# Expert routing and expert loop of one hybrid layer: fused sum on VectorE, pair sums beside the scores, a reordered loop

## The chip, the cores and the metric

One Trainium2 chip, and of it one core. The metric is the device time of one execution in microseconds (us). The core's engines run their own instruction streams in order: TensorE (PE, with its weight loads PEld), VectorE (DVE), ScalarE (ACT), GpSimd (POOL) and SyncE (SP, which here issues most loads). They wait for each other by semaphores.

## What is computed

One layer: an input projection into three groups of heads, an output projection, and then a product-key expert network (PEER) over 512 tokens, d = 1024, 16384 experts. The change lies in the last part alone. Cut to it, the reference is

```python
q = (t @ w_q).reshape(n_tok, 8, 2, 128)                      # 8 heads, two halves
s = einsum('thid,hikd->thik', q, sub_keys)                   # scores against 128 keys per half
v1, i1 = top_k(s[:, :, 0], 16); v2, i2 = top_k(s[:, :, 1], 16)
cand = v1[..., :, None] + v2[..., None, :]                   # 256 sums per head
top_s, pos = top_k(cand, 16)
idx = (i1 * 128 + i2) at pos                                 # 128 experts per token
g = softmax(top_s)
act = gelu(einsum('tkd,td->tk', u_tab[idx], x))
out = einsum('tk,tkd->td', g * act, v_tab[idx])
```

followed by a gated residual and an RMSNorm.

## The kernel before, in words

The 512 tokens are four tiles of 128. Tile 3 gathers its expert rows: 128 times, an indirect DMA issued by GpSimd (`g_load`, L1511) brings one row of u and v (2048 numbers) to each of 128 partitions; DVE takes the dot with the token (`g_dot`, L1516), ACT the gelu of that column (`g_act`, L1519), DVE multiplies the column by the gate (`g_weight`, L1522: wG), ACT scales the v half by it (L1526) and GpSimd adds it to `accG` (L1528). The buffers `row` are four.

Tiles 0 to 2 (384 tokens) take the dense way: for each of 128 groups of 128 experts ("an expert" below) PE computes a u block of 24 matmuls over 384 columns (`u_block`, tile pu), ACT the gelu, DVE multiplies by the dense gate weights gd (L1684), and PE adds the v products, 18 matmuls over 512 columns, into six PSUM accumulators (`e_v`, tile pv). To keep precision each f32 operand is split: ACT copies the high part (`wh`, L177), another engine subtracts to get the low part (`wl`, L180), and three matmuls replace one (L187 to L189). `wwh` and `wwl` are the parts of the weighted activations. 70 of the 128 u blocks, the list `AHEAD`, are computed before the loop: two with the norm, nine beside the scores, and the others by the generator `ahead_steps`, which is stepped by `go_ahead` and from inside the weights stage. Their activations go to DRAM (`act_d`) and come back as `acl`. At depth 2 a step loads and splits pieces up to two steps ahead and issues low parts a step later; the engine of the low parts is `u_eng`, GpSimd until L1617 sets it to DVE.

The stages, in order. Scores: for 16 half heads `hi`, PE computes queries and scores, DVE takes the best 16 per tile (`top16`: MAX8, FIND_INDEX8, MATCH_REPLACE8, twice). In this stage PE and GpSimd follow the written order, and a scheduler places the other engines' instructions. From there on everything follows the written order. Routing: for the tiles 3, 0, 1, 2 the pair sums (`top_pairs`: seven small sums over all eight heads into `cand`, then a `top16` per head), then `route`, which turns positions into expert indices by wide comparisons and products (tiles eq and sel, 128x2048), with the Exp of the softmax on ACT (L1459); seven steps of `ahead_steps` per tile stand between, and two after. Weights: 48 rounds (`weights_T`), in which DVE makes masks (oi, ow), PE multiplies them into gate weights (768 matmuls of 128 columns, gdps), ACT copies these out, and in 36 of the rounds a step of `ahead_steps` is taken; 12 rows of the gather lie here. Expert loop: step i issues the loads of expert i + 4, the dot, gelu and gate of a row, splits u of i + 2 and v of i + 1, computes the u block of i + 1 and weights it, then the row's sum, then the v products of i. 116 rows lie here.

Of the kernel before, what the change touches and what calls it, by code (L numbers as in the profile page):

```python
# [17 lines left out]
P = 128  # L18
# [132 lines left out]
def build(tc, A, out, dbg=None):  # L151
# [1057 lines left out]
    FIRST = [(0, 1), (1, 0), (1, 1), (2, 0)]  # L1209
# [136 lines left out]
    tk = tkp.sb("tk1", side="right")  # L1346
    scp = Pools()
# [40 lines left out]
    def top_pairs(t):  # L1388

        cd = cds[t % 2]  # L1390
        v1, v2 = vv_[t][:, :, 0, :], vv_[t][:, :, 1, :]

        def block(c0, nj, j1, n0, n):

            o = cd[:, :, c0:c0 + 16 * nj].rearrange("p h (j n) -> p h j n", n=16)[:, :, :, n0:n0 + n]
            V.tensor_tensor(o, v2[:, :, n0:n0 + n].unsqueeze(2).broadcast_to([P, 8, nj, n]),
                            v1[:, :, j1:j1 + nj].unsqueeze(3).broadcast_to([P, 8, nj, n]), ALU.add)

        def row(c0, j1, n0, n):
            V.tensor_tensor(cd[:, :, c0:c0 + n], v2[:, :, n0:n0 + n], v1[:, :, j1:j1 + 1].broadcast_to([P, 8, n]), ALU.add)  # L1400
# [6 lines left out]
        V.tensor_tensor(cd[:, :, 128:136], v1[:, :, 8:16], v2[:, :, 0:1].broadcast_to([P, 8, 8]), ALU.add)  # L1407
        for hh in range(8):
            top16(ts_a[t][:, hh, :], pos_a[t][:, hh, :], cd[:, hh, :], 136, tk2)

    psO = scp.ps("psO2", bufs=3)
# [33 lines left out]
    order.enter_context(tc.manual_schedule())  # L1445
    u_depth[0] = 2
    rtp = Pools()
    tk2 = rtp.sb("tk2", bufs=2, side="right")
# [3 lines left out]
    def route(t):  # L1452
# [6 lines left out]
        S.activation(e, e, AF.Exp)  # L1459
# [14 lines left out]
        for i, jj in ((0, j1), (1, j2)):  # L1474
# [14 lines left out]
            if i == 0:  # L1489
                yield  # L1490
# [29 lines left out]

    def g_weight(k):
        V.tensor_tensor(wG[:, k:k + 1], actG[:, k:k + 1], gG[:, k:k + 1], ALU.mult)  # L1522

    def g_acc(k):
        row = rows.pop(k)
        S.activation(row[:, D:2 * D], row[:, D:2 * D], AF.Copy, scale=wG[:, k:k + 1])  # L1526
        if k:
            G.tensor_tensor(accG, accG, row[:, D:2 * D], ALU.add)  # L1528
        else:
            G.tensor_copy(accG, row[:, D:2 * D])  # L1530
# [18 lines left out]
    def weights_T(t):  # L1549
        for q8 in range(16):  # L1550
# [66 lines left out]
    u_eng[0] = V  # L1617
# [26 lines left out]
    ac, ww, gw, sqs, fss = {}, {}, {}, {}, {}  # L1644

    def e_load(a):
        if a in AHEAD:
            ac[a] = gl.tile([P, TD], F32, name="acl")
            nc.sync.dma_start(ac[a], act_d[AHEAD.index(a)])
        elif (a, 0) not in ld:  # L1650
            e_fetch(a, 0)
        if (a, 1) not in ld:
            e_fetch(a, 1)

    def e_split_u(a):
        if (a, 0) not in sp:
            e_split(a, 0)

    def e_split_v(a):
        if (a, 1) not in sp:  # L1660
            e_split(a, 1)
# [175 lines left out]
```

## Time and profile before

| what | us |
|---|---|
| median of three runs (2030.21 to 2032.35) | 2030.38 |
| the profiled execution | 2030.01 |
| its span, first to last instruction | 2028.2 |
| PE busy in the span | 1887.1 (93%) |
| DVE busy | 1516.8 (75%) |
| ACT busy | 932.7 (46%) |
| GpSimd busy | 914.9 (45%) |
| mean granted clock of TensorE | 0.972 of full speed |

The trace gives start and length of each instruction, and for an idle time the event that ended it. A matmul's length is modelled, and matmuls overlap in the pipeline, so the distance from one start to the next tells their pace. The chain of work that ended last lies by 36% on PE, by 29% on DVE and by 17% on issue, time in which an engine waited for nothing that the profile shows.

### The profile page before, as it was taken

How to read it: one execution, taken by the hardware profiler on the slowest of the kernel's cores; microseconds unless marked ns; L12 is line 12 of the kernel's file. 1: busy time of each engine (PE TensorE's matmuls, PEld its weight loads, DVE VectorE, ACT ScalarE, POOL GpSimd, SP SyncE). 2: the span in 40 equal slices, each digit the busy share in tenths (PEclk: the TensorE clock that was granted, in tenths of full speed). 3: DMA queues.
4: the chain of work that ended last, by engine and by line, in shares of the span. 5: the costliest groups of instructions: out<-in, count | busy, mean ns of one | idle time of the engine just before them, and what ended most of it. 6: DMA issues, size and time to landing. Idle time of an engine off the chain costs nothing.

```text
span 2028.2 us, 26813 instructions
## 1 busy us (share of the span) xinstructions
PE 1887.1 (93%) x9703; PEld 1546.4 (76%) x9703; DVE 1516.8 (75%) x2604; ACT 932.7 (46%) x1491; POOL 914.9 (45%) x458
## 2 busy tenths in 40 slices
PE   7999998879998999888999799999999999999997
PEld 4777866556777889888999677777787878778775
DVE  5552179986535456998899878888888888888885
ACT  4332233426544333433777645455445445444444
POOL 1004046740013543564122256576666575675653
PEclk9999999989999999989999789999999999999999
DMA  9546232145313433464787698888888998888971
GB/s 339 166 135 206 63 114 63 42 153 185 96 65 107 147 113 107 132 229 136 246 291 281 230 381 308 313 311 315 304 318 316 354 330 303 317 318 294 323 268 59
DMA packets 209044, 445.20 MB, mean 220 GB/s; under 512 B 13296, under 2 KB 135920, under 8 KB 190960
## 3 DMA queue, kind: packets, MB, share of 16 engines
q1 hardware_dynamic: 171616, 258.47, 39.0%
q0 software_dynamic: 18432, 134.23, 17.4%
q10 hardware_dynamic: 18864, 50.80, 6.7%
q8 instruction: 76, 1.25, 0.2%
q14 instruction: 56, 0.46, 0.1%
HBM read 394.02 MB, written 51.51 MB: 220 GB/s over the span
## 4 chain that ended last, share of the span: by engine, by line
PE 36%; DVE 29%; issue 17%; ACT 8%; DMA 6%; POOL 3%; ACTq 0%; DVEq 0%; SPq 0%; POOLq 0%
DVE wl L180 10%; DVE row L1516 6%; PE acc L187 4%; PE acc L189 4%; PE acc L188 4%; PE pu L189 3%; PE pu L187 3%; PE pu L188 3%; POOL wl L180 3%; ACT wwh L177 3%; DMA wraw<-in_peer_ut 2%; DVE oi L1557 2%; ACT wh L177 2%; DVE ow L1561 1%; PE acc L419 1%
## 5 line engine op out<-in xcount | busy, mean ns | idle before, releaser
L1528 POOL TENSOR_TENSOR accG<-accG,row 128x1024 f32<-128x1024 f32 x127 | 358.7, 2825 | 383.8 <-ACT row L1526 379.3
L180 DVE TENSOR_TENSOR wl<-wraw,wh 128x1024 fp32r<-128x1024 f32 x268 | 339.5, 1283 | 149.0 <-ACT wh L177 140.4
L177 ACT ACTIVATE wh<-wraw 128x1024 fp32r<-128x1024 f32 x324 | 335.1, 1051 | 227.3 <-PE acc L188 80.0
L189 PE MATMUL pu<-u2h,wl 128*128 128x384 f32 (+2 forms) x1040 | 360.9, 347 | 15.1 <-DVE wl L180 12.7
L187 PE MATMUL pu<-u2h,wh 128*128 128x384 f32 (+2 forms) x1040 | 359.3, 346 | 16.0 <-ACT act L1303 14.6
L188 PE MATMUL pu<-u2l,wh 128*128 128x384 f32 (+2 forms) x1040 | 354.8, 341 | 0.0
L187 PE MATMUL pv<-wh,wwh 128*128 128x512 f32 x768 | 310.0, 404 | 25.1 <-ACT wwh L177 24.8
L189 PE MATMUL pv<-wh,wwl 128*128 128x512 f32 x768 | 309.7, 403 | 0.0
L188 PE MATMUL pv<-wl,wwh 128*128 128x512 f32 x768 | 303.7, 395 | 0.0
L1522 DVE TENSOR_TENSOR wG<-actG,gG 128x1 f32<-128x1 f32 x128 | 223.2, 1744 | 33.0 <-ACT actG L1519 33.0
L1511 POOL DMA_INDIRECT row<-in_peer_uv,idxG x128 | 210.9, 1648 | 36.2 <-POOL accG L1528 33.1
L189 PEld LDWEIGHTS pu<-u2h,wl 128*128 128x128 f32 x1040 | 199.8, 192 | 32.2 <-DVE wl L180 28.1
L180 POOL TENSOR_TENSOR wl<-wraw,wh 128x1024 fp32r<-128x1024 f32 x56 | 143.7, 2570 | 166.3 <-ACT wh L177 139.6
L187 PEld LDWEIGHTS pu<-u2h,wh 128*128 128x128 f32 x1040 | 200.3, 193 | 20.2 <-ACT act L1303 15.9
L187 PEld LDWEIGHTS pv<-wh,wwh 128*128 128x128 f32 x768 | 144.9, 189 | 76.6 <-ACT wwh L177 49.7
L188 PEld LDWEIGHTS pu<-u2l,wh 128*128 128x128 f32 x1040 | 200.2, 193 | 2.5
L189 PEld LDWEIGHTS pv<-wh,wwl 128*128 128x128 f32 x768 | 144.7, 188 | 48.5 <-DVE wwl L180 16.6
L188 PEld LDWEIGHTS pv<-wl,wwh 128*128 128x128 f32 x768 | 144.9, 189 | 29.6 <-issue 0.2
L1516 DVE CUSTOM_DVE_ANT_0 row<-row,u2G 128x1024 f32<-128x1024 f32 x128 | 156.1, 1219 | 0.0
L1526 ACT ACTIVATE row<-row,wG 128x1024 f32<-128x1024 f32 x128 | 145.7, 1138 | 4.7 <-ACT act L1303 3.8
L177 ACT ACTIVATE wwh<-acl 128x384 fp32r<-128x384 f32 x70 | 36.7, 525 | 197.0 <-DVE acl L1684 197.0
L1571 ACT ACTIVATE stg<-gdps 128x512 f32<-128x512 f32 x96 | 96.8, 1137 | 17.7 <-PE gdps L1569 17.3
(412 smaller groups left out, 3346.0 us busy)
## 6 DMA issues: line engine op xcount, KB each, us to landing
wraw<-in_peer_ut SPq DMA_DIRECT2D x128, 512.0 KB, 4.6
wraw<-in_peer_uv SPq DMA_DIRECT2D x128, 512.0 KB, 6.3
gd_d<-stg ACTq DMA_DIRECT2D x12, 2048.0 KB, 8.4
gd<-gd_d SPq DMA_DIRECT2D x31, 768.0 KB, 9.1
wraw<-in_w_in SPq DMA_DIRECT2D x36, 512.0 KB, 4.1
acl<-act_d SPq DMA_DIRECT2D x70, 192.0 KB, 5.6
act_d<-act ACTq DMA_DIRECT2D x68, 192.0 KB, 3.8
kT<-in_ada_w SPq DMA_DIRECT2D x18, 512.0 KB, 4.6
```

Of the source, the lines that this page charges most:

```text
L177: S.activation(hi, full, AF.Copy)
L180: (eng or V).tensor_tensor(lo, full, hi.bitcast(F32), ALU.subtract)
L187: PE.matmul(ps, ah, bh, start=start, stop=False)
L188: PE.matmul(ps, ah, bl, start=False, stop=False)
L189: PE.matmul(ps, al, bh, start=False, stop=stop)
L1511: G.indirect_dma_start(out=rows[k], out_offset=None, in_=A["peer_uv"], in_offset=bass.IndirectOffsetOnAxis(ap=idxG[:, k:k + 1], axis=0))
L1516: V.tensor_tensor_reduce(row[:, 0:D], row[:, 0:D], u2G, 1.0, 0.0, ALU.mult, ALU.add, actG[:, k:k + 1])
L1522: V.tensor_tensor(wG[:, k:k + 1], actG[:, k:k + 1], gG[:, k:k + 1], ALU.mult)
L1526: S.activation(row[:, D:2 * D], row[:, D:2 * D], AF.Copy, scale=wG[:, k:k + 1])
L1528: G.tensor_tensor(accG, accG, row[:, D:2 * D], ALU.add)
L1557: V.tensor_tensor(oi.rearrange("p w g b c -> p (w g) b c"), iotaA.unsqueeze(1).broadcast_to([P, 8, P, 2]), tb(ixT), ALU.is_equal)
L1571: S.activation(stg[:, :, t0:t0 + 4].rearrange("p a t -> p t a"), ps, AF.Copy, scale=1.0 / GSCALE)
```

## The change

Four things are changed. The row's sum: ACT makes wG as a scaled copy, and DVE one fused multiply-add into `accG`; ACT's scaling of the row and GpSimd's addition are gone. The pair sums: `top_pairs` works on a group of heads, and the table `PAIRS` puts four, then two heads of each tile behind later scores; the last two heads follow the scores, with one u block per tile; the buffers `sc` are four instead of three. The low parts: `u_eng` becomes DVE right behind those last pair sums (26 low parts change engine), the Exp is issued after the first half of `route`, and three steps of `ahead_steps` per tile are left out of the routing's loop (22 u blocks stand in the routing instead of 30, and 37 in the weights stage instead of 29). The expert loop: loads run six (u) and four (v) experts ahead, gate weights five, u is split three ahead and its block computed two ahead; the high parts are issued first, then the low parts, and the row's gelu and sum stand behind them.

```diff
-    FIRST = [(0, 1), (1, 0), (1, 1), (2, 0)]
+    FIRST = [(1, 0), (0, 1), (3, 0), (1, 1)]
...
         for t in range(NX):
             top16(vv_[t][:, hh, i, :], ix_[t][:, hh, i, :], sc[:, t, :], P, sc2)
+        if hi in PAIRS:
+            for t, h0, nh in PAIRS[hi]:
+                top_pairs(t, h0, nh)
...
+    PAIRS = {8: [(3, 0, 4)], 9: [(0, 0, 4)], 10: [(1, 0, 4)], 11: [(2, 0, 4)],
+             12: [(3, 4, 2)], 13: [(0, 4, 2)], 14: [(1, 4, 2), (2, 4, 2)]}
...
     u_depth[0] = 2
+    for t in (3, 0, 1, 2):
+        top_pairs(t, 6, 2)
+        go_ahead(1)
+    u_eng[0] = V
...
         V.tensor_tensor(e, ts, ts[:, :, 0:1].broadcast_to([P, 8, 16]), ALU.subtract)
-        S.activation(e, e, AF.Exp)
...
             if i == 0:
+                S.activation(e, e, AF.Exp)
                 yield
...
     def g_act(k):
         S.activation(actG[:, k:k + 1], actG[:, k:k + 1], AF.Gelu)
-
-    def g_weight(k):
-        V.tensor_tensor(wG[:, k:k + 1], actG[:, k:k + 1], gG[:, k:k + 1], ALU.mult)
+        S.activation(wG[:, k:k + 1], actG[:, k:k + 1], AF.Copy, scale=gG[:, k:k + 1])
 
     def g_acc(k):
         row = rows.pop(k)
-        S.activation(row[:, D:2 * D], row[:, D:2 * D], AF.Copy, scale=wG[:, k:k + 1])
         if k:
-            G.tensor_tensor(accG, accG, row[:, D:2 * D], ALU.add)
+            V.scalar_tensor_tensor(accG, row[:, D:2 * D], wG[:, k:k + 1], accG, ALU.mult, ALU.add)
...
     for t in (3, 0, 1, 2):
-        go_ahead(3)
-        top_pairs(t)
         r = route(t)
         next(r)
         go_ahead(2)
...
-        for i in range(-4, P + 1):
-            within(e_load, i + 4)
-            if i > -2:
-                within(e_weights, i + 2)
+        for i in range(-6, P + 1):
+            within(lambda a: e_load(a, 0), i + 6)
+            within(lambda a: e_load(a, 1), i + 4)
+            if i > -5:
+                within(e_weights, i + 5)
             now = range(kG[i], kG[i + 1]) if 0 <= i < P else ()
+            within(e_w, i + 1)
             for k in now:
                 g_dot(k)
+            within(lambda a: e_high(a, 0), i + 3)
+            within(lambda a: e_high(a, 1), i + 1)
+            within(lambda a: e_low(a, 2), i + 1)
+            within(lambda a: e_low(a, 0), i + 3)
+            within(lambda a: e_low(a, 1), i + 1)
+            for k in now:
                 g_act(k)
-                g_weight(k)
-            within(e_split_u, i + 2)
-            within(e_split_v, i + 1)
-            within(e_u, i + 1)
-            within(e_w, i + 1)
+            within(e_u, i + 2)
             for k in now:
                 g_acc(k)
                 g_load(k + 4)
```

DVE in the middle of the expert loop, two steps of the loop, before and after (wl is a low part of u or v, wwl one of the weighted activations, the ISA rows are the dot):

```order
L180 TENSOR_TENSOR wl<-wraw,wh 128x1024
L1684 TENSOR_TENSOR act<-act,gd 128x384
L180 TENSOR_TENSOR wwl<-act,wwh 128x384
L1516 ISA row,actG<-row,u2G 128x1024
L1516 ISA actG 128x1
L1522 TENSOR_TENSOR wG<-actG,gG 128x1
L180 TENSOR_TENSOR wl<-wraw,wh 128x1024 x2
L1684 TENSOR_TENSOR acl<-acl,gd 128x384
L180 TENSOR_TENSOR wwl<-acl,wwh 128x384
```

```order
L1688 TENSOR_TENSOR act<-act,gd 128x384
L1530 ISA row,actG<-row,u2G 128x1024
L1530 ISA actG 128x1
L180 TENSOR_TENSOR wwl<-act,wwh 128x384
L180 TENSOR_TENSOR wl<-wraw,wh 128x1024 x2
L1539 SCALAR_TENSOR_TENSOR accG<-row,wG,accG 128x1024
L1688 TENSOR_TENSOR acl<-acl,gd 128x384
L1530 ISA row,actG<-row,u2G 128x1024
L1530 ISA actG 128x1
L180 TENSOR_TENSOR wwl<-acl,wwh 128x384
```

The dot moved between the multiply and wwl, the low parts stand behind wwl, and the fused sum behind them.

DVE at the start of the routing of tile 3, before and after (e is the input of the Exp, j the positions, wl the low part of a u block):

```order
L1458 TENSOR_TENSOR e<-ts_5290 128x128
L1463 CAST pf<-pos_5294 128x128
L1465 TENSOR_SCALAR a4i<-pos_5294 128x128
L1467 TENSOR_SCALAR a15i<-pos_5294 128x128
L1469 SCALAR_TENSOR_TENSOR j_6859<-pf,a4i 128x128
L1471 SCALAR_TENSOR_TENSOR j_6861<-pf,a15i 128x128
L1476 CAST it<-ix_5284 128x128
L1478 TENSOR_TENSOR eq<-iota_5271,j_6859 128x2048
```

```order
L1472 TENSOR_TENSOR e<-ts_5293 128x128
L1476 CAST pf<-pos_5297 128x128
L1478 TENSOR_SCALAR a4i<-pos_5297 128x128
L1480 TENSOR_SCALAR a15i<-pos_5297 128x128
L1482 SCALAR_TENSOR_TENSOR j_7113<-pf,a4i 128x128
L1484 SCALAR_TENSOR_TENSOR j_7115<-pf,a15i 128x128
L180 TENSOR_TENSOR wl<-wraw,wh 128x1024
L1489 CAST it<-ix_5287 128x128
L1491 TENSOR_TENSOR eq<-iota_5274,j_7113 128x2048
```

The first low part of a u block on DVE stands here, behind all the pair sums and six index operations; two more stand between the two halves of `route`.

## Rows read from the trace of the kernel before

**Rows 1.** By stage: window, length, busy PE/PEld/DVE/ACT/POOL (count), PEclk, DMA share, GB/s.

```profile
802.00:957.00 155.00, 137.59 (x727) 134.30 (x725) 146.51 (x412) 57.39 (x78) 83.28 (x33) 0.92 0.51 162
957.00:1115.00 158.00, 148.40 (x1185) 141.67 (x1186) 144.14 (x160) 116.44 (x141) 30.58 (x16) 0.99 0.74 267
1115.00:1168.00 53.00, 36.90 (x303) 32.45 (x302) 44.08 (x51) 35.35 (x41) 15.67 (x9) 0.76 0.63 237
1168.00:2016.00 848.00, 816.92 (x3676) 665.94 (x3676) 713.18 (x799) 415.77 (x617) 533.83 (x239) 0.99 0.85 304
1168.00:1184.00 16.00, 12.72 (x46) 10.05 (x47) 10.64 (x14) 5.97 (x10) 4.30 (x3) 0.82 1.01 411
```

**Rows 2.** Timeline of PE in the expert loop: start us, length us, engine, line, operation.

```profile
1500.92 0.34 PE L187 MATMUL pu<-u2h,wh 128*128 128x384 f32 x1
...
1504.62 0.40 PE L187 MATMUL pv<-wh,wwh 128*128 128x512 f32 x1
...
1508.59 0.40 PE L189 MATMUL pv<-wh,wwl 128*128 128x512 f32 x1
```

**Rows 3.** Timeline of DVE there; in brackets idle time ahead and its releaser.

```profile
1504.75 2.00 DVE L1522 TENSOR_TENSOR wG<-actG,gG 128x1 f32<-128x1 f32 x1 [0.27 <-ACT actG L1519]
1506.68 1.21 DVE L180 TENSOR_TENSOR wl<-wraw,wh 128x1024 fp32r<-128x1024 f32 x1
1507.81 0.55 DVE L1684 TENSOR_TENSOR act<-act,gd 128x384 f32<-128x384 f32 x1
1508.95 0.56 DVE L180 TENSOR_TENSOR wwl<-act,wwh 128x384 fp32r<-128x384 f32 x1 [0.59 <-ACT wwh L177]
1509.42 1.22 DVE L1516 CUSTOM_DVE_ANT_0 row<-row,u2G 128x1024 f32<-128x1024 f32 x1
...
1520.16 1.21 DVE L180 TENSOR_TENSOR wl<-wraw,wh 128x1024 fp32r<-128x1024 f32 x1
```

**Rows 4.** Timeline of GpSimd (POOL) in the same stretch.

```profile
1503.87 2.86 POOL L1528 TENSOR_TENSOR accG<-accG,row 128x1024 f32<-128x1024 f32 x1 [2.46 <-ACT row L1526]
1507.00 1.71 POOL L1511 DMA_INDIRECT row<-in_peer_uv,idxG  x1 [0.27 <-POOL accG L1528]
```

**Rows 5.** Waits in the routing: who for whom, us in total, times, longest.

```profile
ACT e L1459 <- DVE e L1458: 26.5, 4, 8.6
PEld pu L187 <- ACT act L1303: 15.9, 4, 6.3
```

**Rows 6.** Tile eq in the routing: count, shortest/median/longest ns, first and last start.

```profile
L1484 DVE TENSOR_TENSOR eq<-sel x16: 291/693/2776, 826.9 to 950.3; 128x1024 f16<-128x1024 f16 x8, 128x256 f16<-128x256 f16 x8
...
L1480 DVE TENSOR_TENSOR sel<-eq,it x8: 1224/3263/3307, 823.6 to 945.8; 128x2048 f16<-128x2048 f16 x8
L1484 DVE TENSOR_TENSOR sel<-eq x8: 425/1454/2517, 829.8 to 949.8; 128x512 f16<-128x512 f16 x8
```

**Rows 7.** Timeline of DVE in the scores and the first pair sums.

```profile
741.75 0.49 DVE L1362 MAX8 v<-sc 128x8 f32<-128x128 f32 x2 [1.47 <-ACT sc L1381]
...
746.50 0.29 DVE L1366 FIND_INDEX8 ix<-v,s 128x8 uint32<-128x128 f32 x1
...
806.52 0.28 DVE L1396 TENSOR_TENSOR cand<-v 128x120 f32<-128x120 f32 x1
...
808.13 0.31 DVE L1362 MAX8 ts<-cand 128x8 f32<-128x136 f32 x1
...
821.07 0.27 DVE L1458 TENSOR_TENSOR e<-ts 128x128 f32<-128x128 f32 x1
```

**Rows 8.** Groups in the weights stage: count, busy us, mean ns, idle ahead.

```profile
L1557 DVE TENSOR_TENSOR oi<-iotaA,ixT 128x2048 f16<-128x2048 f16 x48 | 74.1, 1543 | 0.0
```

**Rows 9.** Timeline of PE in the weights stage, fifteen short matmuls in a row.

```profile
1140.26 0.22 PE L1569 MATMUL gdps<-ow,oi 128*128 128x128 f16 x1 [0.37 <-DVE ow L1561]
...
1141.07 0.22 PE L1569 MATMUL gdps<-ow,oi 128*128 128x128 f16 x1
```

**Rows 10.** Line 585, a fused multiply-add over 770 elements early in the program.

```profile
L585 DVE SCALAR_TENSOR_TENSOR c<-xp,colv,c x12: 1015/1022/1023, 66.0 to 171.1; 128x770 f32<-128x770 f32 x12
```

More of the change, by code (lines that the diff above doesn't have):

```diff
@@ L1346, in build @@
     tk = tkp.sb("tk1", side="right")
+    rtp = Pools()
+    tk2 = rtp.sb("tk2", bufs=2, side="right")
     scp = Pools()
@@ L1406, in top_pairs @@
         row(66, 4, 2, 1)
-        V.tensor_tensor(cd[:, :, 128:136], v1[:, :, 8:16], v2[:, :, 0:1].broadcast_to([P, 8, 8]), ALU.add)
-        for hh in range(8):
-            top16(ts_a[t][:, hh, :], pos_a[t][:, hh, :], cd[:, hh, :], 136, tk2)
+        V.tensor_tensor(cd[:, :, 128:136], v1[:, :, 8:16], v2[:, :, 0:1].broadcast_to([P, nh, 8]), ALU.add)
+        for hh in range(nh):
+            top16(ts_a[t][:, h0 + hh, :], pos_a[t][:, h0 + hh, :], cd[:, hh, :], 136, tk2)
+    PAIRS = {8: [(3, 0, 4)], 9: [(0, 0, 4)], 10: [(1, 0, 4)], 11: [(2, 0, 4)],
+             12: [(3, 4, 2)], 13: [(0, 4, 2)], 14: [(1, 4, 2), (2, 4, 2)]}
     psO = scp.ps("psO2", bufs=3)
@@ L1445, in build, with go_ahead @@
     order.enter_context(tc.manual_schedule())
+    def go_ahead(n):
+        for _ in range(n):
+            next(ahead, None)
     u_depth[0] = 2
-    rtp = Pools()
-    tk2 = rtp.sb("tk2", bufs=2, side="right")
+    for t in (3, 0, 1, 2):
+        top_pairs(t, 6, 2)
+        go_ahead(1)
+    u_eng[0] = V
     slots = {}
@@ L1584, in weights_T @@
                 g_act(k)
-            elif q8 % 4 == 3:
-                g_weight(k)
     UQ = (0, 1, 3, 4, 5, 7, 8, 9, 11, 12, 13, 15)
-    def go_ahead(n):
-        for _ in range(n):
-            next(ahead, None)
     def whole(gen):
@@ L1616, in build @@
     slots_T(2)
-    u_eng[0] = V
     rtp.close()
@@ L1643, in build, with e_load, e_high, e_low @@
     accT = [[psV.tile([P, 512], F32, name=f"pv{t}{hf}") for hf in range(2)] for t in range(3)]
-    ac, ww, gw, sqs, fss = {}, {}, {}, {}, {}
-    def e_load(a):
-        if a in AHEAD:
+    ac, ww, sqs, fss = {}, {}, {}, {}
+    def e_load(a, i):
+        if i == 0 and a in AHEAD:
             ac[a] = gl.tile([P, TD], F32, name="acl")
             nc.sync.dma_start(ac[a], act_d[AHEAD.index(a)])
[L1650 to L1661, printed above, removed]
+        elif (a, i) not in ld:
+            e_fetch(a, i)
+    def e_high(a, i):
+        if (a, i) in ld and (a, i) not in sp:
+            lows[a, i] = []
+            e_split(a, i, None, lows[a, i])
+    def e_low(a, i):
+        for f in lows.pop((a, i), ()):
+            f()
+    lows = {}
+    gds = {}
     def e_weights(a):
@@ L1683, in e_w @@
         xq = x.rearrange("p (q t) -> p q t", q=NQ)
-        V.tensor_tensor(xq, xq, gw.pop(a), ALU.mult)
+        V.tensor_tensor(xq, xq, gds[a // 4][:, :, a % 4 * TQ:(a % 4 + 1) * TQ], ALU.mult)
         wh = ex.tile([P, TD], F32R, name="wwh", bufs=3)
         wl = ex.tile([P, TD], F32R, name="wwl", bufs=3)
-        split(wh, wl, x)
+        lows[a, 2] = []
+        split(wh, wl, x, None, lows[a, 2])
         ww[a] = (wh, wl)
@@ L1746, in build @@
     LAST = 3
-    kG = [12 + min(P - 12, (i * (P - 12) + 121) // 122) for i in range(P + 1)]
+    kG = [12 + min(P - 12, (i * (P - 12) + 120) // 121) for i in range(P + 1)]
     with tc.manual_schedule():
```

23 lines of the change are left out of this document (10 added, 13 removed).

## The prediction

> **What bounds the kernel now.** I read the stages first, then the pace of TensorE (PE) inside the longest one, then what stands beside it there. The busy time by stage [rows 1] cuts the end of the program into routing (802 to 957 us), weights (957 to 1168) and the expert loop (1168 to 2016). PE is busy for nearly all of each, but a busy PE is not PE at its peak, so its pace is read from start to start. In a stretch without stalls [rows 2], 21 steps of a u block take 1504.62 - 1500.92 = 3.70 us, 0.176 us each, and 17 steps of the v products take 3.97 us, 0.2335 us each. The expert loop holds 58 u blocks of 24 matmuls and 128 experts of 18 v matmuls: 58 x 24 x 0.176 + 128 x 18 x 0.2335 = 245 + 538 = 783 us. It lasts 848. So 65 us of it are not PE's own work.
>
> VectorE (DVE) takes them. Its rows [rows 3] show two experts, one with a u block and one whose activations are loaded, from one low part at 1506.68 to the like one at 1520.16: 13.48 us. PE needs 24 x 0.176 + 36 x 0.2335 = 4.22 + 8.41 = 12.63 us for the same two. The loop thus runs at DVE's in-order chain. The reader should look at one DVE row above all: wG, 128x1 elements, takes 2.00 us from 1504.75, and ends as GpSimd's accG addition ends (1503.87 + 2.86 = 1506.73, [rows 4]). A multiply of one column is held, inside the instruction, by GpSimd's addition. The idle times ahead of wwl (0.59 us, for ACT's high part) and wG (0.27 us, for the gelu) lengthen the chain too [rows 3].
>
> In the routing DVE is busy for 146.5 of 155 us [rows 1], and much of it is held as well: the product over 2048 takes 3.26 us in the median where its shortest is 1.22, the sums over 1024 and less reach 2.78 us [rows 6]. GpSimd is busy then for 83 us [rows 1], with the low parts of the u blocks. PE loses 16 us in four waits behind ACT, which stands at an Exp whose input DVE has not made (26.5 us) [rows 5]. In the weights stage DVE is busy 188 of 211 us, and in the last 53 us, where u blocks run out, PE is busy for 37, at 0.76 of its clock in the mean of its two levels, 1.2 and 2.4 GHz [rows 1].
>
> **The expert loop: what goes.** GpSimd's 127 additions and ACT's 128 scalings go; DVE gets one fused multiply-add of 128x1024 per row; the 128x1 multiply goes to ACT. On DVE two experts with two rows then need three low parts (3 x 1.21), two multiplies by the weights (2 x 0.55), two wwl (2 x 0.56), two dots (2 x 1.22) and two fused sums. The trace has no fused sum of this size. From below, the dot with two inputs of 1024 takes 1.22 us [rows 3]; from above, the same operation over 770 elements takes 1.021 us [rows 10], in proportion 1.36 for 1024. I take 1.29, midway, since a part of the 1.021 is a fixed start. Sum: 3.63 + 1.10 + 1.12 + 2.44 + 2.58 = 10.9 us against PE's 12.63; at 1.36 it is 11.0. The two waits on ACT lose their place as well: the dot now stands between the multiply and wwl, and the low parts between the gelu and the fused sum. So DVE is no longer the slower one, and PE's 783 us become the bound. What is late next? The u block is computed two experts ahead and split three ahead, so a DVE round can start when the u block of the round before is done, and has a whole v block as slack; loads are issued six and four experts ahead, so a transfer should not take the wait's place. I add 12 us for the start of the loop and the stalls that remain: 795 us, **53 us less**. ACT's added 128x1 operation is small beside the scaling that it loses, and ACT is busy for 416 of 848 us [rows 1].
>
> A sum on GpSimd held DVE; the gather stays on GpSimd. Does it hold DVE too? The multiply at 1507.81 started within the gather's 1.71 us (1507.00 to 1508.71) and took its 0.55 us [rows 3, 4]. So no. The Trainium skill ("SBUF — State Buffer", section "SBUF: two separate sides") says that VectorE and GpSimd share a port pair as an exclusive lock, which whoever starts first keeps for the whole instruction, against a VectorE operation with two SBUF inputs if the GpSimd one reads SBUF. Read strictly, a gather that reads its indices there would hold the new sums; the 0.55 us row speaks against it. The third rival below has the price.
>
> **The routing.** 6 of 8 heads of the pair work move up beside the scores. There DVE has room only in part. From the ninth set of scores at 741.75 it has eight sets of 5.04 us (to 746.50 + 0.29), 40 us [rows 7]. All 32 heads of pairs are still to come; eight in a row cost 13.0 us (808.13 to 821.07), or 1.26 a head where they overlap as the four tiles of a set do: 40 to 52 us, I take 46. Their small sums, 12 narrower groups in place of 4 of 1.6 us (806.52 to 808.13), make about 14, and being held by GpSimd's low parts 0 to 12, of which I take 6. DVE is through at 741.75 + 40 + 46 + 14 + 6 = 848, while PE's scores end at 802. Who is queued behind? From here on low parts stand on DVE, in order behind the pairs. Six u blocks, split before the switch, still have theirs from GpSimd: 6 x 4.22 = 25 us, to 827. The seventh waits for the pairs, for 1.6 us of index arithmetic (six operations like e at 0.27) and for its 1.21 us low part: 851. **PE stalls 24 us**, once (13 to 36 with the ends above), in place of the four waits behind Exp, which now stands behind work that DVE has done. From then on GpSimd adds nothing there, so the wide operations run at their shortest [rows 6]: per tile 2 x (1.22 + 1.22 + 0.69 + 0.43 + 0.29 + 0.29) = 8.3 us and about 3 of small ones, with four low parts 16.1 us, against 4 x 4.22 = 16.9 of PE. PE sets the pace again. The stage computes 22 blocks where it had 30: 24 + 22 x 4.22 = 117 us instead of 155, **38 us less**.
>
> **The weights.** They inherit 8 blocks. PE: 37 x 4.22 = 156 us, and 768 short matmuls of 0.058 us (14 steps in 0.81 us, [rows 9]) are 44.5, together 201. DVE: 188 busy now; it loses 48 x (1.54 - 1.22) = 15 us of holding in the masks [rows 6, 8] and gains 8 low parts and 12 fused sums, 25 us: 198, or 213 if the holding stays. The two are level; I allow 8 us for waits between them and take 209 where it was 211, **2 us less**. The eight blocks cost almost nothing here: they fill the last 53 us, in which PE waited and its clock fell.
>
> **Sum.** 2028.2 - 38 - 2 - 53 = 1935 us of span; the profiled execution took 2030.0 for its span of 2028.2, so add 1.8: **1937 us**. The median of the runs, 2030.4, is 0.4 above that execution, which I leave aside. The tail after 2016 isn't touched.
>
> **Rivals.** First, the expert loop stays where it is because transfers take DVE's place. For it: the DMA engines' share is 0.85 at 304 GB/s, and 848/795 asks for 324. Against: in the first 16 us of the loop they moved 411 GB/s [rows 1]. If 304 is the roof, the 53 us are lost: 1990. Chance 0.10. Second, DVE's lag out of the scores is twice as large, as its small sums are held there, and the weights become DVE's at 219: 1937 + 24 + 10 = 1971. Against it: what stands between those sums, MAX8 and its kin, runs at even length in [rows 7]. Chance 0.12. Third, on the other side: the gather holds each fused sum for its 1.71 us. In the mean of the loop two experts have 2.84 low parts and 1.81 rows: 10.2 us of DVE, + 1.81 x 1.71 = 13.3, and, DVE being the bound again, the waits on ACT as now (2 x 0.59 + 1.81 x 0.27 = 1.7): 15.0 x 64 = 960 us, 112 more than today against 40 saved ahead: 2102. It makes the kernel slower from (848 + 40)/64 = 13.9 us a pair, so from 1.1 us of holding a sum. For it: the 2.00 us of wG; against it the 0.55 us. Chance 0.05. Fourth, the reordering gives only half of its slack, and half of the loop's gain stays out: 1964, chance 0.08.
>
> **Chances.** The forecast, with 1912 to 1962 of its own, gets 0.60; the remaining 0.05 goes to a better end, where the stall is 13 us and nothing is lost between engines: 2030 - 49 - 10 - 65 = 1906. From 1908 to 1985 the range leaves out the first and third rival and most of the better end, about 0.2. Faster by over 0.2% (what a measurement of this kernel tells from no change): 0.93, same 0.02, slower 0.05.
>
> **What would show it.** Right: no DVE instruction of one column at 2 us; fused sums of 1.2 to 1.4 us; in the expert loop starts of PE at 0.176 and 0.2335 us with few waits for wwh or wl, and DVE idle ahead of its multiply, waiting for gelu; one PE wait of 13 to 36 us for a DVE low part near 830; weights that end near 1130 without a hole, at the full clock. Wrong: fused sums over 2.3 us, waits for wraw or row in the expert loop, or a PE that waits for DVE in every weights step.

## The result, and the profile after

The changed kernel takes 1940.59 us (median of four runs, 1938.96 to 1943.0) where the kernel before took 2030.78 on the same chip: a ratio of 0.9556, with an interval of 0.9539 to 0.9572. Predicted were 1937 us and a range of 1908 to 1985. The profiled execution has a span of 1937.1 us. The forecast of the total held. Its parts did not all hold; that their errors cancelled is luck.

Four marks cut the end of both traces: PE's last matmul of the scores, DVE's first mask `oi`, the first and the last start of PE in `pv`. The stages are read from one profiled execution of each kernel.

| stage, us | before | change predicted | after | change measured |
|---|---|---|---|---|
| up to the end of the scores | 801.3 | 0 | 801.1 | -0.2 |
| routing | 156.6 | -38 | 108.1 | -48.5 |
| weights, up to the first v product | 211.4 | -2 | 234.1 | +22.7 |
| expert loop | 846.0 | -53 | 781.4 | -64.6 |
| tail | 12.9 | 0 | 12.4 | -0.5 |

The stages of the changed kernel by windows, with the columns of [rows 1]; then the first lines of its page (share of the span and count of each engine, and the chain that ended last, by engine):

```profile
802.00:909.00 107.00, 95.59 (x534) 94.60 (x532) 94.03 (x308) 45.90 (x65) 11.69 (x7) 0.95 0.52 181
909.00:1125.00 216.00, 199.04 (x1602) 190.34 (x1603) 184.67 (x216) 147.20 (x186) 18.44 (x11) 0.99 0.74 273
1143.00:1925.00 782.00, 781.24 (x3676) 675.68 (x3676) 621.22 (x797) 321.66 (x617) 121.62 (x122) 1.00 0.88 324
```

```profile
PE 1835.8 (95%) x9703; PEld 1545.1 (80%) x9703; DVE 1400.2 (72%) x2686; ACT 829.5 (43%) x1491; POOL 404.7 (21%) x304
...
PE 71%; DVE 17%; ACT 6%; issue 3%; DMA 2%; ACTq 0%; POOL 0%; SPq 0%; DVEq 0%; POOLq 0%
```

In the expert loop PE is busy for 781 of 782 us at the full clock; in [rows 1] it was 817 of 848. DVE there fell from 713 to 621 us, and it now waits for the gelu of the u block. This is DVE's timeline for two experts (start, length, engine, line, operation; in brackets idle time and its releaser), to be held against [rows 3]:

```profile
1503.81 0.56 DVE L1688 TENSOR_TENSOR act<-act,gd 128x384 f32<-128x384 f32 x1 [2.48 <-ACT act L1682]
1504.29 1.22 DVE L1530 CUSTOM_DVE_ANT_0 row<-row,u2G 128x1024 f32<-128x1024 f32 x1
...
1505.43 0.56 DVE L180 TENSOR_TENSOR wwl<-act,wwh 128x384 fp32r<-128x384 f32 x1
1505.91 2.36 DVE L180 TENSOR_TENSOR wl<-wraw,wh 128x1024 fp32r<-128x1024 f32 x2
1508.19 1.27 DVE L1539 SCALAR_TENSOR_TENSOR accG<-row,wG,accG 128x1024 f32<-128x1024 f32 x1
```

The 0.59 us ahead of wwl are gone, the one-column multiply is gone, the fused sum takes 1.27 us, and 2.48 us of idle time stand ahead of the multiply. In the loop as a whole (waits between 1150 and 1915 us: who for whom, us in total, times, longest):

```profile
ACT act L1682 <- PE pu L189: 226.7, 57, 5.6
...
DVE act L1688 <- ACT act L1682: 142.3, 57, 4.9
...
DVE wwl L180 <- ACT wwh L177: 10.1, 12, 3.3
```

ACT waits for PE, DVE for ACT, and no wait of PE is among the first rows: PE is the bound.

### The profile page after: what moved, and what is told of

The parts are those of the page before. It is cut to its first block, busy times and chain, and to the rows that moved or that the text cites. A ratio compares the mean times of both kernels' runs of the same rounds, so it can differ in the third digit from the quotient of the medians.

```text
span 1937.1 us, 26349 instructions
## 1 busy us (share of the span) xinstructions
PE 1835.8 (95%) x9703; PEld 1545.1 (80%) x9703; DVE 1400.2 (72%) x2686; ACT 829.5 (43%) x1491; POOL 404.7 (21%) x304
## 4 chain that ended last, share of the span: by engine, by line
PE 71%; DVE 17%; ACT 6%; issue 3%; DMA 2%; ACTq 0%; POOL 0%; SPq 0%; DVEq 0%; POOLq 0%
PE pv L188 9%; PE pv L189 9%; PE pv L187 9%; PE pu L187 7%; PE pu L189 6%; PE pu L188 6%; PE acc L187 3%; PE acc L188 3%; PE acc L189 3%; ACT stg L1582 2%; DVE wl L180 2%; PE acc L419 2%; PE acc L421 1%; PE acc L423 1%; PE po L1049 1%
## 5 line engine op out<-in xcount | busy, mean ns | idle before, releaser
L180 DVE TENSOR_TENSOR wl<-wraw,wh 128x1024 fp32r<-128x1024 f32 x294 | 362.9, 1252 | 167.4 <-ACT wh L177 167.1
L189 PE MATMUL pu<-u2h,wl 128*128 128x384 f32 (+2 forms) x1040 | 352.2, 339 | 12.6 <-DVE wl L180 12.5
L1525 POOL DMA_INDIRECT row<-in_peer_uv,idxG x128 | 133.4, 1042 | 899.7 <-DVE accG L1539 781.3
L187 PE MATMUL pv<-wh,wwh 128*128 128x512 f32 x768 | 304.2, 396 | 5.1 <-ACT wh L177 5.1
L189 PE MATMUL pv<-wh,wwl 128*128 128x512 f32 x768 | 303.9, 396 | 0.0
L1539 DVE SCALAR_TENSOR_TENSOR accG<-row,wG,accG 128x1024 f32<-128x1024 f32 x127 | 162.4, 1279 | 0.0
L1688 DVE TENSOR_TENSOR act<-act,gd 128x384 f32<-128x384 f32 x58 | 33.5, 578 | 142.4 <-ACT act L1682 142.3
L1682 ACT ACTIVATE act<-pu 128x384 f32<-128x384 f32 x58 | 28.5, 491 | 227.1 <-PE pu L189 226.7
L180 POOL TENSOR_TENSOR wl<-wraw,wh 128x1024 fp32r<-128x1024 f32 x30 | 72.1, 2404 | 106.9 <-ACT wh L177 88.4
## 6 DMA issues: line engine op xcount, KB each, us to landing
gd<-gd_d SPq DMA_DIRECT2D x31, 768.0 KB, 12.4
```

The costliest lines, as they stand in the source:

```text
L180: (eng or V).tensor_tensor(lo, full, hi.bitcast(F32), ALU.subtract)
L187: PE.matmul(ps, ah, bh, start=start, stop=False)
L189: PE.matmul(ps, al, bh, start=False, stop=stop)
L1525: G.indirect_dma_start(out=rows[k], out_offset=None, in_=A["peer_uv"], in_offset=bass.IndirectOffsetOnAxis(ap=idxG[:, k:k + 1], axis=0))
L1539: V.scalar_tensor_tensor(accG, row[:, D:2 * D], wG[:, k:k + 1], accG, ALU.mult, ALU.add)
L1682: S.activation(ac[a], pu[:, :TD], AF.Gelu)
```

## The experiments

A run's time is the median of its executions, and each ratio is to the kernel before on the same chip, with its interval. This table holds the stages of every run, cut by the same marks, each from one profiled execution (the changed kernel has two, which differ by 0.3 us).

| run | what it is | routing | weights | loop | ratio |
|---|---|---|---|---|---|
| before | | 156.6 | 211.4 | 846.0 | 1 |
| after | | 108.1 | 234.1 | 781.4 | 0.9556 |
| e1_sum | before + fused sum | 156.6 | 222.1 | 897.8 | 1.0324 [1.0306, 1.0342] |
| e2_loop | before + reordered loop | 156.6 | 211.2 | 780.7 | 0.9690 [0.9669, 0.9712] |
| e3_wact | before + wG on ACT | 155.5 | 213.6 | 840.1 | 0.9981 [0.9970, 0.9991] |
| e4_route | before + routing part | 108.0 | 237.7 | 839.9 | 0.9868 [0.9851, 0.9884] |
| e5_after_again | the changed kernel again | 108.1 | 234.4 | 781.7 | 0.9556 [0.9543, 0.9569] |
| e6_nosum | after, sum back on GpSimd | 108.1 | 230.0 | 778.6 | 0.9526 [0.9513, 0.9539] |
| e7_store | after, two stores moved | 108.0 | 229.8 | 778.6 | 0.9512 [0.9499, 0.9525] |
| e8_sumlate | e1 + gelu behind the splits | 156.3 | 223.0 | 784.1 | 0.9756 [0.9743, 0.9769] |
| e9_late | before + gelu and gate behind the splits | 156.5 | 211.2 | 839.1 | 0.9968 [0.9957, 0.9979] |
| e10_best | e6 + e7 | 108.1 | 231.4 | 778.7 | 0.9516 [0.9495, 0.9536] |
| e11_pairs | e4 without low parts on DVE | 113.7 | 235.8 | 840.1 | 0.9888 [0.9871, 0.9904] |
| e12_lowv | before + low parts on DVE | 163.9 | 211.5 | 845.5 | 1.0031 [1.0020, 1.0042] |

**Which part pays in the loop?** Four runs part the change: the fused sum alone, the reordered loop alone, the moved multiply alone, the routing part alone. The first is e1_sum.

```diff
-        V.tensor_tensor(wG[:, k:k + 1], actG[:, k:k + 1], gG[:, k:k + 1], ALU.mult)
+        S.activation(wG[:, k:k + 1], actG[:, k:k + 1], AF.Copy, scale=gG[:, k:k + 1])
...
-            G.tensor_tensor(accG, accG, row[:, D:2 * D], ALU.add)
+            V.scalar_tensor_tensor(accG, row[:, D:2 * D], wG[:, k:k + 1], accG, ALU.mult, ALU.add)
```

> The kernel before with the fused sum alone (wG on ACT, one multiply-add on DVE, nothing of the sum on GpSimd); order and routing as before. Theory H (GpSimd's addition held DVE's one-column multiply): two experts cost DVE 13.48 - 2 x 2.00 - 2 x 0.27 + 2 x 1.28 = 11.5 us, which is under PE's 12.63, so the expert loop (846 us before from the first to the last v product, 781 after) falls to 785 to 800 and the total to 1970 to 1985. Theory O (the order of the waits was what cost): the 0.59 us waits for wwh and the wait for gelu behind the u block stay, the loop stays above 820 and the total above 2000.

Measured: 2094.11 us, 3.2% slower than before, within the bounds of the second theory. The loop lost 52 us and the weights 11, although nothing holds DVE any more. DVE's timeline in e1_sum, the same columns as above:

```profile
1498.96 1.22 DVE L1516 CUSTOM_DVE_ANT_0 row<-row,u2G 128x1024 f32<-128x1024 f32 x1
...
1501.73 2.36 DVE L180 TENSOR_TENSOR wl<-wraw,wh 128x1024 fp32r<-128x1024 f32 x2 [1.55 <-ACT wh L177]
...
1505.15 0.56 DVE L180 TENSOR_TENSOR wwl<-acl,wwh 128x384 fp32r<-128x384 f32 x1 [0.59 <-ACT wwh L177]
1505.63 1.28 DVE L1525 SCALAR_TENSOR_TENSOR accG<-row,wG,accG 128x1024 f32<-128x1024 f32 x1
...
1513.56 1.22 DVE L1516 CUSTOM_DVE_ANT_0 row<-row,u2G 128x1024 f32<-128x1024 f32 x1
```

and ACT's beside it:

```profile
1500.22 0.20 ACT L1519 ACTIVATE actG<-actG 128x1 f32<-128x1 f32 x1 [2.96 <-DVE actG L1516]
1500.46 0.30 ACT L1520 ACTIVATE wG<-actG,gG 128x1 f32<-128x1 f32 x1
1500.66 1.99 ACT L177 ACTIVATE wh<-wraw 128x1024 fp32r<-128x1024 f32 x2
```

From the dot at 1498.96 to the dot two experts on, 1513.56, DVE takes 14.60 us, where the kernel before took 13.48 and PE needs 12.63. In the old order ACT's gelu of the dot stands ahead of the high parts `wh`. ACT idles 2.96 us for the dot, and then needs 0.20, 0.30 and about 1 us before DVE can begin a low part: 1.55 us lost in each round. In the kernel before, ACT's high part lay beside the 2.00 us for which wG was held (1504.75 to 1506.75, [rows 3]). These are ACT's rows there:

```profile
1504.52 0.20 ACT L1519 ACTIVATE actG<-actG 128x1 f32<-128x1 f32 x1 [0.73 <-DVE actG L1516]
1504.62 1.05 ACT L177 ACTIVATE wh<-wraw 128x1024 fp32r<-128x1024 f32 x1
```

The high part was done at 1505.67, a microsecond before DVE came to its low part at 1506.68. The hold had covered it.

e2_loop has the opposite half: the loop in the new order and with the new, larger leads, with wG on DVE and the sum on GpSimd as before.

```diff
+            within(e_w, i + 1)
             for k in now:
                 g_dot(k)
+            within(lambda a: e_high(a, 0), i + 3)
...
+            within(lambda a: e_low(a, 1), i + 1)
+            for k in now:
                 g_act(k)
                 g_weight(k)
...
-            within(e_u, i + 1)
-            within(e_w, i + 1)
+            within(e_u, i + 2)
```

> The kernel before with the reordered expert loop alone; the sum stays on GpSimd, wG a multiply on DVE, now behind the low parts. Theory H: wG or a neighbour of it is still held for about 2 us a row, DVE needs 3.63 + 1.10 + 1.12 + 2.44 + 2 x 2.0 = 12.3 us for two experts, next to PE's 12.63, so the loop comes to 790 to 815 us and the total to 1975 to 2000. Theory O: the loop is at PE's pace, 781 to 787, total near 1968.

Measured: 1965.97 us; the loop takes 780.7 us, as short as in the full change. Its DVE, and its GpSimd (POOL) beside it:

```profile
1500.43 0.14 DVE L1522 TENSOR_TENSOR wG<-actG,gG 128x1 f32<-128x1 f32 x1
...
1502.26 2.60 DVE L180 TENSOR_TENSOR wwl<-acl,wwh 128x384 fp32r<-128x384 f32 x1
1504.79 1.21 DVE L180 TENSOR_TENSOR wl<-wraw,wh 128x1024 fp32r<-128x1024 f32 x1
...
1507.75 2.61 DVE L180 TENSOR_TENSOR wwl<-act,wwh 128x384 fp32r<-128x384 f32 x1
...
1512.56 0.14 DVE L1522 TENSOR_TENSOR wG<-actG,gG 128x1 f32<-128x1 f32 x1
```

```profile
1501.89 2.55 POOL L1528 TENSOR_TENSOR accG<-accG,row 128x1024 f32<-128x1024 f32 x1 [2.83 <-ACT row L1526]
1504.72 0.97 POOL L1511 DMA_INDIRECT row<-in_peer_uv,idxG  x1 [0.27 <-POOL accG L1528]
```

The hold is still there, and a little longer: wwl takes 2.60 us instead of 0.56, and it is now wwl that is held. But two experts take DVE 1512.56 - 1500.43 = 12.13 us. In the kernel before they took 13.48, of which 2 x 0.59 + 2 x 0.27 = 1.72 were waits on ACT. [rows 3] shows the first wait of 0.59 in these two experts; the others are these rows of the kernel before:

```profile
1510.92 2.01 DVE L1522 TENSOR_TENSOR wG<-actG,gG 128x1 f32<-128x1 f32 x1 [0.27 <-ACT actG L1519]
...
1516.26 0.56 DVE L180 TENSOR_TENSOR wwl<-acl,wwh 128x384 fp32r<-128x384 f32 x1 [0.59 <-ACT wwh L177]
...
1518.23 2.01 DVE L1522 TENSOR_TENSOR wG<-actG,gG 128x1 f32<-128x1 f32 x1 [0.27 <-ACT actG L1519]
```

13.48 - 1.72 = 11.76, and the hold is 0.35 us longer (two wwl of 2.60 and 2.61 where 0.56 is free, two wG of 2.01 where 0.14 is free): 12.11. With the dot between the multiply and wwl, DVE's waits on ACT are gone, DVE is just below PE's 12.63, and the loop is PE's. No run has the dot's new place without the larger leads, so what the leads give here is not shown; e8_sumlate below keeps the old leads, and its loop takes 784.1 us.

e3_wact moves only the one-column multiply to ACT; the sum stays on GpSimd.

```diff
-        V.tensor_tensor(wG[:, k:k + 1], actG[:, k:k + 1], gG[:, k:k + 1], ALU.mult)
+        S.activation(wG[:, k:k + 1], actG[:, k:k + 1], AF.Copy, scale=gG[:, k:k + 1])
```

> The kernel before with one edit: wG is a scaled copy on ACT; the row's scaling and GpSimd's addition stay. If GpSimd's addition holds whatever two-input operation comes, the hold passes on to the low part behind it: low parts of 2 to 3 us, loop 830 to 846, total 2012 to 2030. If the one-column multiply were slow by itself, its 2 us a row are gone, the loop is at PE's 785 to 800 and the total near 1975.

Measured: 2026.46 us, loop 840.1, as the first case has it. One line of DVE's groups in its loop (count, busy us, mean ns, idle ahead and its releaser) shows both halves at once, the hold on the low parts (1605 ns in the mean; in e2_loop, where they are free, 1213) and e1_sum's wait:

```profile
L180 DVE TENSOR_TENSOR wl<-wraw,wh 128x1024 fp32r<-128x1024 f32 x184 | 290.9, 1605 | 194.8 <-ACT wh L177 194.8
```

So an operation that is taken out of GpSimd's way passes the hold to the next one, though not the whole of it: 184 x (1605 - 1213) ns = 72 us are held here, where the 116 wG of the loop before were held for 204 us (1.91 us in the mean, 0.15 free). What DVE gained went into the wait for ACT.

e4_route makes the routing part of the change alone (pair sums beside the scores, later Exp, shorter routing, low parts on DVE).

```diff
+        if hi in PAIRS:
+            for t, h0, nh in PAIRS[hi]:
+                top_pairs(t, h0, nh)
...
+    for t in (3, 0, 1, 2):
+        top_pairs(t, 6, 2)
+        go_ahead(1)
+    u_eng[0] = V
...
-        go_ahead(3)
-        top_pairs(t)
```

> The kernel before with the routing part alone (pair sums beside the scores, low parts on DVE, Exp later, 22 blocks in the routing); sum and expert loop as before. If the stages add up: from the last score to the first mask 156 falls to 108 us, the weights stage up to the first v product rises from 211 to 225 to 235, the expert loop stays at 846: total 2004 to 2012. If the longer weights stage of the changed kernel comes from the fused sums or the new loop's loads, it stays below 218 here and the total is 1985 to 1995.

Measured: 2001.88 us, the first case, somewhat outside its bounds: the weights take 237.7 us, and the loop 839.9, though its code is that of the kernel before; why is not shown. The routing is as short as in the full change, and the weights stage is 26 us longer than before. So the longer weights stage of the result comes with the routing part; it doesn't need the fused sum.

**The order on ACT.** e8_sumlate tests e1_sum's cause: two lines are moved behind the splits.

```diff
             for k in now:
                 g_dot(k)
-                g_act(k)
             within(e_split_u, i + 2)
             within(e_split_v, i + 1)
+            for k in now:
+                g_act(k)
```

> The kernel before with the fused sum, as in the first experiment, and one more edit: the row's gelu and wG stand behind the high parts of u and v on ACT. There each low part waited 1.55 us for a high part that stood behind the gelu of the dot just made. If that order is the whole cause of its 62 us, DVE needs 11.5 to 12.1 us for two experts, the loop falls from 898 to 785 to 805 and the total to 1970 to 1990. If the fused sum is slow for another reason (its own length, the gather's holding), the total stays over 2040.

Measured: 1982.53 us. The loop falls from 897.8 to 784.1 us, and the wait of DVE for `wh` (between 1200 and 1960 us) from 157.7 us to 5.7; DVE waits for the gelu of the u block, as in the changed kernel. The order of two small activations, 128x1 each, was worth 114 us there. e9_late makes the same move with the sum on GpSimd.

> Before, with one change: the gelu of the dot and the one-column multiply stand behind the splits of the high and low parts; the sum stays on GpSimd, the loads and blocks keep their old lead. Theory A: the two lines alone take the dot's gelu out of the high parts' way, as they did under the fused sum (loop 784 us there): loop 783 to 800 us, total 1965 to 1985. Theory B: with the sum on GpSimd a DVE instruction is still held for 2 us a row and the waits for wwh stay (2 x 0.59 us per two experts), so that DVE needs 13.48 - 0.27 = 13.2 us per two experts where it needed 13.48: loop 830 to 848, total 2012 to 2030; the reordered loop then owes its 781 us to the larger lead and to the dot between the multiply and wwl. A reading above 2030 would fit neither.

Measured: 2024.18 us, loop 839.1: the second theory. DVE's rows show why:

```profile
1500.41 0.56 DVE L180 TENSOR_TENSOR wwl<-acl,wwh 128x384 fp32r<-128x384 f32 x1 [0.59 <-ACT wwh L177]
...
1502.41 3.03 DVE L180 TENSOR_TENSOR wl<-wraw,wh 128x1024 fp32r<-128x1024 f32 x1 [0.30 <-ACT wh L177]
...
1508.57 4.19 DVE L180 TENSOR_TENSOR wl<-wraw,wh 128x1024 fp32r<-128x1024 f32 x2 [0.29 <-ACT wh L177]
...
1513.89 0.56 DVE L180 TENSOR_TENSOR wwl<-acl,wwh 128x384 fp32r<-128x384 f32 x1 [0.59 <-ACT wwh L177]
```

Two experts take 1513.89 - 1500.41 = 13.48 us, exactly as before: the hold sits on the low parts, the two waits of 0.59 us remain, and two of 0.3 us for `wh` stand where those of 0.27 for the gelu were. Two ways thus bring DVE below PE: no hold and the gelu behind the splits (e8_sumlate), or the hold with the whole reordering (e2_loop). Either is enough. The change makes both.

**Is the fused sum worth anything?** On one chip, e5_after_again is the changed kernel once more, and e6_nosum the changed kernel with the sum back on GpSimd. This is the edit of e6_nosum against the changed kernel:

```diff
+        S.activation(row[:, D:2 * D], row[:, D:2 * D], AF.Copy, scale=wG[:, k:k + 1])
...
-            V.scalar_tensor_tensor(accG, row[:, D:2 * D], wG[:, k:k + 1], accG, ALU.mult, ALU.add)
+            G.tensor_tensor(accG, accG, row[:, D:2 * D], ALU.add)
```

> The changed kernel once more, on the same chip as the next three: ratio to before near 0.956.

> The changed kernel with the sum put back: wG a multiply on DVE behind the low parts, the row scaled on ACT and added on GpSimd; routing and reordered loop stay. The reordered loop alone ran at PE's pace (781 us) with GpSimd's addition still holding wwl at 2.6 us. If the fused sum is worth nothing once the order is right, this equals the changed kernel within 0.3% (1937 to 1946). If the fused sum gives what the first theory put on it, the loop loses 20 us or more here and the total is over 1957.

Measured: 1940.88 us for the changed kernel and 1934.76 us with the sum on GpSimd. The two intervals do not touch: with the new order, the fused sum costs 6 us. In e6_nosum PE is busy for the whole loop while GpSimd adds for a row at every step (window, same columns as above):

```profile
1143.00:1921.00 778.00, 778.00 (x3674) 673.64 (x3673) 728.14 (x796) 404.31 (x615) 424.95 (x238) 1.00 0.89 325
```

DVE is busy for 728 us with the hold and 621 without, and PE's time does not depend on it. The 6 us lie ahead of the loop and at its start: from the first mask to the last short matmul the weights take 211.0 us instead of 216.8, where 12 fused sums no longer stand on DVE, the stretch from there to the first v product is 1.3 us longer, and the loop is 3.1 us shorter. That the 12 sums are the cause is argued, not shown: no run moves them alone.

**The start of the loop.** In the changed kernel ACT stands there for 9.72 us (timeline of ACT; ACTq is its queue, issuing a store):

```profile
1129.00 0.33 ACTq L1584 DMA_DIRECT2D gd_d<-stg  x1
...
1131.94 0.53 ACT L177 ACTIVATE wwh<-acl 128x384 fp32r<-128x384 f32 x1 [1.13 <-DVE acl L1688]
1141.77 0.37 ACTq L1304 DMA_DIRECT2D act_d<-act  x1
1142.19 1.06 ACT L177 ACTIVATE wh<-wraw 128x1024 fp32r<-128x1024 f32 x1 [9.72 <-DMA gd_d<-stg]
```

The store of a block's activations at 1141.77 goes out only when the 2 MB store of 1129.00 has landed, and the high part of the first v block is queued behind it. PE waits 5.1 us for that part, and the granted clock, 1.00 up to 1138 us, is 0.81 over the wait and 0.72 over the 8.7 us behind it, means of its two levels of 1.2 and 2.4 GHz (windows, same columns):

```profile
1138.00:1143.30 5.30, 0.24 (x3) 0.00 (x1) 0.02 (x1) 1.11 (x2) 0.00 (x0) 0.81 0.92 376
1143.30:1152.00 8.70, 8.23 (x28) 6.55 (x29) 8.65 (x12) 4.91 (x9) 1.04 (x1) 0.72 0.96 330
```

e7_store has GpSimd issue the last two of these stores.

```diff
-            nc.scalar.dma_start(act_d[i], act)
+            (nc.gpsimd if i >= n - 2 else nc.scalar).dma_start(act_d[i], act)
```

> The changed kernel with one edit: the last two stores of activations to DRAM are issued by GpSimd instead of ACT. In the changed kernel ACT stood 9.7 us at such a store, which waited for the 2 MB of gate weights stored before it, and a high part stood behind it. If that wait sets the start of the loop, the distance from the last mask matmul to the first v product falls from 18 to 9 to 11 us and the total by 5 to 9 us. If the loop's start waits for the gate weights themselves, nothing changes.

Measured: 1932.14 us, 8.7 less than the changed kernel. From the last mask matmul to the first v product it takes 12.7 us, not quite the 9 to 11 that were expected, and the loop is 3.1 us shorter. ACT issues `wh` without the wait, and PE goes from u blocks into v products at the full clock:

```profile
1127.00:1140.00 13.00, 13.00 (x85) 13.00 (x83) 5.41 (x6) 7.58 (x11) 3.33 (x4) 1.00 0.86 307
1140.00:1152.00 12.00, 12.00 (x60) 10.61 (x59) 10.91 (x15) 5.86 (x12) 1.58 (x2) 1.00 1.03 384
```

e10_best joins the edits of e6_nosum and e7_store.

> The changed kernel with the row's sum back on GpSimd and the last two stores of the activations issued by GpSimd: the two single edits gained 6.1 and 8.7 us. If they are independent: 1940.7 - 14.8 = 1926. If both shorten the same stretch (the weights stage and the start of the loop, where GpSimd would then have sums, stores and gathers), only the larger stays: 1932. First pv near 1138 us, loop 778 to 779 us.

Measured: 1932.46 us: the two edits do not add up. With the sum on GpSimd the hole has another cause. In e10_best, between 1120 and 1146 us, DVE stands at the weighting of reloaded activations, a low part is queued behind it, and PE waits for that (in e6_nosum the same two waits take 10.5 and 3.5 us):

```profile
DVE acl L1693 <- DMA acl<-act_d: 11.6, 1, 11.6
...
PE pu L189 <- DVE wl L180: 4.7, 1, 4.7
```

e7_store and e10_best are the fastest of all kernels here, and can't be told apart.

**The routing in two halves.** e11_pairs is e4_route without the line that sets `u_eng` ahead of the routing; e12_lowv is the kernel before with that line alone:

```diff
     u_depth[0] = 2
+    u_eng[0] = V
```

> Before, with the pair sums beside the scores, the later Exp and the shorter routing (22 u blocks in it), but the low parts of the u blocks stay on GpSimd until the place where the kernel before changes them. Theory A (the prediction's step): GpSimd's low parts go on holding DVE's wide products and sums, so the routing lasts 120 to 135 us where the whole routing part gave 108, and the total is 2010 to 2025 against 2002. Theory B: the moved pairs alone give the routing's gain, since PE has 22 x 4.22 = 93 us of blocks and DVE, though held, has 4 x 22 = 88: routing 105 to 112, total 2000 to 2006.

> Before, with one line: the engine of the low parts becomes DVE at the start of the routing; the pair sums stay there. Theory A: nothing holds DVE's wide operations any more: 146.5 us busy less 8 to 11 us a tile of holding, plus 30 low parts of 1.22 us = 37: 139 to 151, so the routing stays at 145 to 157 and the total at 2018 to 2032; each part of the routing's gain needs the other. Theory B: PE never waits long and sets the pace, 30 x 4.22 = 127 us: routing 127 to 140, total 2000 to 2015. Theory C: the low parts queue behind 14.6 us of pair sums on DVE, PE waits there in each tile, routing over 160 and the total above 2035.

Measured: 2007.74 us for e11_pairs, between its two theories, and 2038.28 us for e12_lowv, the third of its theories. Without the low parts on DVE the routing takes 113.7 us: 43 of the 48.5 us are there, with DVE still held (the product sel at 3.28 us in the median, as in [rows 6]). The run also has the later Exp, and 8 u blocks fewer in the routing, 34 us of PE's work that went to the weights. How much of the 43 us each of the three gives is not shown: no run moves one alone. The low parts on DVE alone make the routing 7 us longer. DVE is busy for 133 of 163.5 us in e12_lowv, where [rows 1] has 146.5 of 155, and PE waits for it all the same, since the low parts of its u blocks stand in order behind whole tiles of pair sums (first row e12_lowv, 801 to 965 us; second row e11_pairs, 801 to 920 us):

```profile
PE pu L189 <- DVE wl L180: 26.1, 4, 6.5
```

```profile
PE pu L189 <- POOL wl L180: 4.6, 2, 4.2
```

With the pairs moved, the same line is worth 113.7 - 108.0 = 5.7 us.

## Why the prediction was right, point by point

- **What bounds the loop: right.** PE's 783 us were its floor, DVE's in-order chain held it above, and the new loop takes 781.4. The 12 us added for stalls were not needed, which is most of the difference between 53 and 64.6.
- **Which part of the chain: wrong.** The prediction looked "above all" at the held multiply. Its sum of 10.9 us for two experts takes out both the hold and the waits on ACT, so its total did not depend on which of them counts. The hold was there, as read, but e2_loop keeps it and is as fast, and e1_sum takes it away and is slower. The step that failed is that an instruction which is held was counted as lost time; ACT's work for the next low part lay beside it. What the reordering took was the 1.72 us of waits on ACT per two experts, which the prediction names second ("lengthen the chain too").
- **The size of the fused sum: right.** 1.29 us were taken, 1.28 measured (127 of them):

```profile
L1539 DVE SCALAR_TENSOR_TENSOR accG<-row,wG,accG 128x1024 f32<-128x1024 f32 x127 | 162.4, 1279 | 0.0
```

- **The routing: mechanism right, two terms off.** DVE reaches the e of tile 3 at 834.7 us, not 848, so that PE's one stall is 10.0 us where 24 were taken, below the 13 to 36 given for it. What follows runs free, as said: the product sel at 1.22 us, against 3.26 in [rows 6]. These are the wait, and the row of the tile (shortest, median, longest ns):

```profile
PE pu L189 <- DVE wl L180: 10.0, 1, 10.0
```

```profile
L1493 DVE TENSOR_TENSOR sel<-eq,it x8: 1224/1224/1226, 838.4 to 896.2; 128x2048 f16<-128x2048 f16 x8
```

But e11_pairs shows that the free operations were worth 6 us; the rest goes with the shorter PE work (8 blocks of 4.22 us, 34 us, went to the weights), the later Exp and the pairs that no longer stand in the way, which no run parts.
- **The weights: mis-sized.** The term is the "8 us for waits between them", the engines. PE's own 201 us were right (37 blocks and 768 short matmuls), DVE has 184.7 + 3.9 us instead of 198, the masks run at 1.22 us, and the stage takes 234.1: 33 us more than PE's work. Before, by the same reckoning, PE had 29 x 4.22 + 44.5 = 167 of 211 us, so 44 were lost. Eight blocks of 34 us recovered only 11 of these. The clock was read rightly: 0.76 in the last 53 us before, it is 0.99 in the mean of the stage up to 1125 us. Of the 33, e7_store takes off 4.6 and e6_nosum 4.4, but e10_best with both edits only 3.0, so these are not two separate parts. The others lie between PE, DVE and ACT, each waiting for another (waits from 909 to 1125 us); no run parts them, and they stay open.

```profile
ACT act L1303 <- PE pu L189: 32.8, 24, 3.4
DVE wl L180 <- ACT wh L177: 29.7, 11, 4.4
ACT stg L1582 <- PE gdps L1580: 21.6, 13, 3.4
...
PE gdps L1579 <- DVE ow L1572: 13.9, 12, 3.5
```

Routing and weights belong together: predicted -40, measured -25.8, and the loop's extra 11.6 us made up for most of it.
- **"Without a hole, at the full clock": wrong.** The hole of 1138 to 1143 us came from a store on ACT's queue that the prediction left out.
- **The rivals.** Transfers: the loop asked for 324 GB/s, as worked out, and got it; e2_loop got 329. A larger lag of DVE: it was smaller. Half of the slack lost: no. The gather that holds the fused sum: no. The 116 fused sums of the loop take 1.275 to 1.282 us; none of them begins within a gather, since the gather waits for the row that the sum frees. In the changed kernel the 116 dots of the loop take 1.219 us in the mean, and the 60 of them that began within a gather 1.218; in e2_loop's rows the low part that starts at 1504.79, within the gather from 1504.72, takes its 1.21 us. The Trainium skill ("SBUF — State Buffer", section "SBUF: two separate sides") gives the port pair for the whole instruction to whichever of the two engines starts first; the additions agree (wwl 2.60 us), and the gather, if it is counted as such an instruction, does not.

## What to carry to other kernels

In this loop a held instruction on the limiting engine was no loss as long as work of another engine hid beside it: before removing a hold, list what runs during it and ask who would wait next. Put small dependent operations of an in-order engine behind those that feed the bound engine; here, with the fused sum, the place of a 128x1 gelu and a 128x1 copy was worth 114 us, and with the sum on GpSimd (e9_late) 7. When work is moved into a stage that seems to have room, count the waits between engines that the stage already shows as part of its length: of 44 us here, 33 stayed.

## What the hardware showed unexpectedly

The hold by GpSimd's addition is not bound to an instruction: it took wG (2.00 us, [rows 3]), wwl (2.60 us, e2_loop), or a low part (3.03 us, e9_late), whichever two-input DVE instruction came up while the addition ran. The hold also works the other way. In the loop before, the 6 additions that began while DVE ran nothing took 2.41 us in the mean; the 110 that began during a dot took 2.87, and ended 2.27 us after that dot. The gather waits as well. It takes 1.71 us in [rows 4], where a low part on DVE ran on for 0.89 us after its start, and 0.97 us in e2_loop, where wwl ran on for 0.14. In the loops of before, after, e1_sum, e2_loop, e6_nosum, e8_sumlate and e9_late alike, a gather that begins during a two-input DVE instruction ends 0.81 to 0.83 us after that instruction in the mean, whether this ran on for 0.15 us or for 0.88, and one that begins while DVE runs nothing takes 0.94 to 0.96 us. So the traces show the gather waiting for a running DVE instruction, without holding a later one. No run was made to test it.
